# Pieces of each scan group laid between the next group's projection units, and the residual gate's matrix-vector product moved into the first half of the output projection

## The chip, the cores and the metric

The kernel runs on one core of a Trainium2 chip. The metric is the device time of one execution in microseconds (us). One core has five instruction streams, each executed in order: PE (TensorE, matrix products), DVE (VectorE), ACT (ScalarE), POOL (GpSimd) and SP (SyncE, which here only issues DMA transfers). Engines wait for each other by semaphores.

## The reference, cut to what matters

One layer with 512 latent tokens, 256 context tokens and model width 2048. The normalised, modulated input goes through one projection; its columns feed a windowed attention (16 heads) and a bidirectional Mamba-2 scan (16 heads in 4 groups, chunks of 128 tokens). Both results are normalised, multiplied by one output matrix, scaled by a residual gate and added to the input.

```python
shift, scale, gate = jnp.split((jax.nn.silu(c) @ w_mod + b_mod)[:, None, :], 3, axis=-1)
px = (rmsnorm(x, norm_g) * (1 + scale) + shift) @ w_in
...
# scan, per group and direction
cb = jnp.einsum('bclgn,bcsgn->bgcls', cc, bc)
wts = cb[:, :, None] * jnp.exp(segsum(a_t))
y_diag = jnp.einsum('bgrcls,bcsgrp->bclgrp', wts, xdt)
states = jnp.einsum('bclgn,bgrcl,bclgrp->bcgrpn', bc, decay_states, xdt)
...
y_off = jnp.einsum('bclgn,bcgrpn,bgrcl->bclgrp', cc, prev, jnp.exp(a_cs))
...
h = jnp.concatenate([rmsnorm(att * jax.nn.silu(g_att), att_norm_g), rmsnorm(y * jax.nn.silu(z), ssd_norm_g)], axis=-1)
x = x + gate * (h @ w_out)
```

`gate` is one row of 2048 numbers: a vector of 2048 times a matrix of 2048 x 2048 (16 MB in float32).

## The kernel before, in words

**Products.** Every float32 operand is split in two parts, hi and lo, and a product is three matrix multiplications (hi by hi, lo by hi, hi by lo), all through the helper of L49. All elementwise operations of two tensors go through L55.

**Streamed units.** The input projection is cut into units of 128 output columns. `load_unit` (L298) loads a unit's weights in two halves (tile `wr`, 512 KB each); ACT takes the hi part (`wh`, L308) and DVE the lo part (`wl`, L55). `proj` (L316) multiplies 16 blocks by 512 latent tokens (`pj`, 48 matmuls) and, where the unit is wanted for the context, by 256 context tokens (`pjc`, 48 more). In the names `pj_13` or `wr_13_0` the first number is the unit. Unit 0 is the last eighth of the scan's output gate z; units 1 to 16 are the four scan groups (x0, x1, B, C each; C without context); 17 and 18 are the keys, the rest queries and attention gates.

**Scan groups.** `ssd_group` (L474) is called four times. It projects the group's four units, convolves them (`conv_silu`), and then: transposes x and B to token layout (`xtp`, `btp`, to `xtok`, `btok`); forms the chunk states (`stc`, `stx`, with `xw` and `stt` on DVE); forms `cbp`; and, for two pairs of heads, the state term `z` and the diagonal term `yps`. In front of a `yps` stands a chain: a row of running sums is loaded onto all partitions (tile `df`, 256 KB, from `csd` in HBM), ACT takes its exponential (`ec`), DVE the masked differences (L566, four per row), ACT the exponential (L569) and a scaling (L573), DVE the sum of both directions (L575, four) and the product with `cb`. `yps` multiplies the result by `xtok`. The pairs are numbered 0 to 7; `yps_5` is the second pair of group 2.

**Order.** A scheduler lays the instructions of each engine in an order by priorities. Loads and splitting of weights have a raised priority (`HP_W`), as have `df` loads (`HB`) and convolutions, so the next group's projection matmuls come between the pieces of a scan group as far as the scheduler's own order brings them.

**Residual gate.** `gate_step` (L274) is called four times per unit in units 2 to 17. Each call loads one block of 128 x 512 of the gate's weights (tile `wg`, 256 KB, one buffer) and DVE adds the product with the conditioning vector to `ga` (L290). After 16 blocks `gp` sums `ga` over the partitions (a 1 x 512 matmul result), and the row goes to HBM (`grow`). In the output projection it is loaded back onto all partitions (`gate`).

**Output projection.** It has two halves: half 1 (scan's columns of h) first, then half 0 (attention's). In each half four column blocks n of 512 are made; a block loads four `wo` tiles (512 KB, eight k steps of 128), splits them into `woh` and `wol`, and does 12 matmuls per k step into four token tiles (`o_half_n_t`, 96 matmuls a block). Half 1 leaves `part = o * rsum`. After block n of half 1, `add_x` (L799) on POOL makes `part * gate + x` of block n-1, with four `xo` loads of x. Half 0 then makes `o * rsum * gate` (L879) and adds it to `part` on DVE. `finish_half` (L642) of the attention's half (squares on ACT, `hfu` on DVE, `hacc` and `hal` on POOL) runs beside the first block of half 1.

Of the kernel before, what the change touches and what calls it, by code (L numbers as in the profile page):

```python
# [43 lines left out]
def emit(tc, xin, ctxT, wmod, wgate, bgate, wz, wvd, wu, wo, fng, vecs, cst, rope, out, dbg=None):  # L44
# [18 lines left out]
    with es:  # L63
# [24 lines left out]
        # persistent activations: transposed normalised inputs in two exact parts  # L88
# [27 lines left out]
        def rms_rows(o, acc, n, tag):  # L116
            """1 / rms of every token, on all partitions, from the sums of squares per partition."""
# [13 lines left out]
        def load_latent():  # L131
            """Latent tokens: transposed as they come, in column blocks; 1 / rms of every token on all partitions."""
# [44 lines left out]
        # silu of the two modulation vectors, zero-padded to one column group  # L177
# [90 lines left out]
        dp = es.enter_context(tc.tile_pool(name="dp", bufs=1, space=bass.MemoryType.DRAM))  # L268
        grow = dp.tile([1, D], F32, name="grow")
        gsteps = iter(range(4 * KT))  # L270
        gacc = []
        geng = nc.vector

        def gate_step(ld):  # L274
            """One k block of 512 gate columns: products per partition, summed over partitions after the last."""
            i = next(gsteps, None)
            if i is None:
                return
            n, k = divmod(i, KT)
            if k == 0:  # L280
                ga = wp.tile([P, 512], F32, tag="ga", name=f"ga_{n}", bufs=1)
                gacc.append(ga)
                nc.gpsimd.memset(ga, 0.0)
                with tc.issue_after(ld.ins):
                    nc.sync.dma_start(ga[0:1, :], bgate[:, n * 512:(n + 1) * 512])
            ga = gacc[n]
            wg = wp.tile([P, 512], F32, tag="wg", name=f"wg_{n}_{k}", bufs=GB)
            with tc.issue_after(ld.ins):
                nc.sync.dma_start(wg, wgate[n, k])
            geng.scalar_tensor_tensor(out=ga, in0=wg, scalar=sc0[:, k:k + 1], in1=ga, op0=ALU.mult, op1=ALU.add)  # L290
            if k == KT - 1:
                gp = bank("tp", f"gp_{n}", shape=(1, 512))
                mm(gp, ones[:, 0:1], ga, True, True)
                nc.scalar.activation(ga[0:1, :], gp, AF.Copy)
                nc.sync.dma_start(grow[:, n * 512:(n + 1) * 512], ga[0:1, :])

# [1 line left out]
        def load_unit(u, ctxp=False):  # L298
            """Yields (k, hi, lo) weight blocks [128, 128] of unit u."""
            for hf in range(2):  # L300
                with tc.high_priority(HP_W):
                    wr = wp.tile([P, 8, P], F32, tag="wr", name=f"wr_{u}_{hf}", bufs=WR)
                    ld = nc.sync.dma_start(wr, wu[u, :, hf * 8:hf * 8 + 8, :])
                for qf in range(2):
# [6 lines left out]
                    if 2 <= u < 18:  # L311
                        gate_step(ld)
# [3 lines left out]
        def proj(u, with_ctx):  # L316
# [72 lines left out]
        z7, _ = proj(0, False)  # L389
        stmp = sp.tile([P, S], F32, tag="stmp", name="stmp_7")  # L390
        silu2(z7, yT[7], stmp)
        st.close()

# [35 lines left out]
        da = w2("da", "sm", 4, fl)  # L429
# [13 lines left out]
        dd = w2("dd", "sm", 4, fl)  # L443
# [6 lines left out]
        csx = w2("csx", "sm", 4, [P, NT, 2, 16])  # L450
# [8 lines left out]
        def conv_silu(pa, pb, ci, o):  # L459
            """Depthwise conv of width 3 and silu: pa [128, n] in PSUM -> o in SBUF."""  # L460
# [13 lines left out]
        def ssd_group(g, units):  # L474
            ux0, ux1, ub, uc = units
            xs = []
            for i, u in enumerate((ux0, ux1)):
                a, b = proj(u, True)
                o = w2(f"xs_{g}_{i}", "xs", 3, (P, S + CT))
                conv_silu(a, b, 2 * g + i, o)  # L480
                xs.append(o)
            a, b = proj(ub, True)
            bT = w2(f"bT_{g}", "xs", 3, (P, S + CT))
            conv_silu(a, b, 8 + g, bT)
            a, _ = proj(uc, False)
            cT = w2(f"cT_{g}", "cT", 1)
            conv_silu(a, None, 12 + g, cT)

            xtok = w2(f"xtok_{g}", "xtok", 1, (P, 6, 256))
# [32 lines left out]
            for stp in range(3):  # L522
                for d in range(2):
# [7 lines left out]
                    tt(nc.vector, stt_[d][:, nx, :], stt_[d][:, nx, :], sp_, ALU.add)  # L531

            cbp = bank("tp", f"cbp_{g}")
            for c in range(NT):
                cc = slice(c * P, (c + 1) * P)
                mm(cbp[:, cc], bT[:, cc], cT[:, cc], True, True)
            cb = w2(f"cb_{g}", "cb", 1)
            nc.scalar.activation(cb, cbp, AF.Copy, scale=0.25)

            for pr in range(2):  # L540
                tix = 2 * g + pr
                # state term of both heads at once: exp(cs) scales it afterwards
                zs = []
                for d in range(2):
                    z = bank("sa", f"z_{tix}_{d}")
                    for c in range(NT):
                        cc = slice(c * P, (c + 1) * P)
                        mm(z[:, cc], stt_[d][:, c, pr * P:(pr + 1) * P], cT[:, cc], True, True)
                    zs.append(z)
                ecs = [w2(f"ec_{tix}_{d}", "ec", 3) for d in range(2)]  # L550
                yps = bank("pv", f"yps_{tix}")
                dm = []
                for hh in range(2):
                    r = tix * 2 + hh
                    hr = slice(hh * 64, hh * 64 + 64)
                    dx = []
                    for d in range(2):
# [3 lines left out]
                        with tc.high_priority(HB):  # L561
                            nc.sync.dma_start(df, csd[d * 16 + r].partition_broadcast(P))
# [447 lines left out]
```

## Time and profile before

| what | value |
|---|---|
| time before, median of 3 runs (lowest, highest) | 1056.57 us (1055.89, 1059.32) |
| span of the profiled execution | 1054.8 us |
| PE busy | 1009.6 us (96%) |
| DVE busy | 722.0 us (68%) |
| ACT busy | 494.6 us (47%) |
| POOL busy | 173.5 us (16%) |
| moved by DMA | 143.25 MB |

The span of the profiled execution is its own time, from its first instruction to its last; no other time is shown for that execution, and the median of the three runs is 1.8 us above it. In the rows below a group of instructions reads: line, engine, operation, result <- operands, shape and count, then busy time and the mean duration in ns, then the idle time of the engine just before the instructions of this group and what ended it. Matmuls overlap on PE, so one lasts longer than the distance from it to the next.

### The profile page before, as it was taken

The page shows a single profiled execution, that of the slowest core. Times are in us where ns is not written, and L with a number is a line of the kernel's source. Part 1 is how long each engine was busy: PE and PEld are TensorE (multiplying, and loading weights), DVE is VectorE, ACT ScalarE, POOL GpSimd, SP SyncE. Part 2 cuts the span into 40 slices and gives each one's busy share as a digit, 9 for nine tenths or more (in the row PEclk, how much of TensorE's full clock was granted, in tenths as well). Part 3 has the DMA queues.
Part 4 walks back from the last instruction along what each step waited for, and adds up shares of the span by engine and source line. Part 5 has one row for each costly group of instructions (what it writes and reads, how often), then busy time and mean ns, then how long its engine had stood idle before and what let it go on. Part 6 is the DMA issues. An engine that isn't in the chain of part 4 may idle for free.

```text
span 1054.8 us, 15524 instructions
## 1 busy us (share of the span) xinstructions
PE 1009.6 (96%) x5682; PEld 818.7 (78%) x5682; DVE 722.0 (68%) x1474; ACT 494.6 (47%) x1064; POOL 173.5 (16%) x120
## 2 busy tenths in 40 slices
PE   5999999999999989989989999999999998999996
PEld 4677789788778868868868777777777777888885
DVE  4332378585875985885889888788798866333765
ACT  6222275263352453263345567666666655333333
POOL 1232200000210110110037100000000008744220
PEclk9999999999999999989999999999999999999998
DMA  9999963354244244444331211112111135442304
GB/s 333 385 347 348 343 212 95 110 165 147 70 120 145 92 149 125 112 120 139 120 107 56 84 61 42 59 40 80 41 40 61 61 99 221 151 167 91 100 33 160
DMA packets 50845, 143.25 MB, mean 136 GB/s; under 512 B 5544, under 2 KB 5928, under 8 KB 50512
## 3 DMA queue, kind: packets, MB, share of 16 engines
q1 hardware_dynamic: 50768, 142.25, 40.5%
q8 instruction: 45, 0.74, 0.3%
q14 instruction: 32, 0.26, 0.1%
HBM read 137.96 MB, written 4.27 MB: 135 GB/s over the span
## 4 chain that ended last, share of the span: by engine, by line
PE 61%; DVE 12%; DMA 5%; ACT 3%; issue 3%; POOL 1%; SPq 0%; ACTq 0%; DVEq 0%; POOLq 0%
PE pj L49 25%; PE o L49 14%; PE pjc L49 5%; PE pv L49 3%; PE ptp L756 3%; PE sl L49 3%; DMA wg<-in_wgate_dram 2%; PE vps L49 2%; DVE df L566 2%; DVE wl L55 2%; DMA df<-csd 2%; PE sc L49 2%; DVE ga L290 1%; DVE df L575 1%; PE stx L49 1%
## 5 line engine op out<-in xcount | busy, mean ns | idle before, releaser
L49 PE MATMUL pj<-xh,wh 128*128 128x512 f32 x560 | 225.5, 403 | 0.0
L49 PE MATMUL pj<-xl,wh 128*128 128x512 f32 x560 | 224.6, 401 | 0.0
L49 PE MATMUL pj<-xh,wl 128*128 128x512 f32 x560 | 224.0, 400 | 0.0
L308 ACT ACTIVATE wh<-wr 128x512 fp32r<-128x512 f32 x140 | 87.9, 630 | 137.5 <-PE pjc L49 66.2
L49 PEld LDWEIGHTS pj<-xh,wl 128*128 128x128 f32 x560 | 105.7, 189 | 21.3 <-issue 0.9
L55 DVE TENSOR_TENSOR wl<-wr,wh 128x512 fp32r<-128x512 f32 x140 | 103.5, 742 | 24.9 <-ACT wh L308 21.0
L49 PEld LDWEIGHTS pj<-xl,wh 128*128 128x128 f32 x560 | 106.4, 190 | 15.1 <-issue 1.9
L49 PEld LDWEIGHTS pj<-xh,wh 128*128 128x128 f32 x560 | 106.5, 190 | 13.9 <-issue 1.0
L55 DVE TENSOR_TENSOR wol<-wo,woh 128x512 fp32r<-128x512 f32 x56 | 53.3, 968 | 63.6 <-ACT woh L846 57.3
L290 DVE SCALAR_TENSOR_TENSOR ga<-wg,sc,ga 128x512 f32<-128x512 f32 x64 | 50.8, 794 | 49.2 <-DMA wg<-in_wgate_dram 48.1
L55 POOL TENSOR_TENSOR ec<-ec,ec 128x512 f32<-128x512 f32 x8 | 11.2, 1397 | 349.2 <-DVE ec L55 328.9
L846 ACT ACTIVATE woh<-wo 128x512 fp32r<-128x512 f32 x56 | 34.8, 630 | 70.8 <-PE o L49 62.3
L55 POOL TENSOR_TENSOR hacc<-hacc,hsq 128x512 f32<-128x512 f32 x14 | 20.4, 1454 | 288.7 <-ACT hsq L654 286.3
L49 PE MATMUL pjc<-chq,wh 128*128 128x256 f32 x224 | 65.2, 291 | 2.1 <-DVE xs L468 2.1
L49 PE MATMUL pjc<-clq,wh 128*128 128x256 f32 x224 | 64.4, 288 | 0.0
L49 PE MATMUL pjc<-chq,wl 128*128 128x256 f32 x224 | 63.7, 284 | 0.0
L760 ACT ACTIVATE ph<-ptp 128x512 fp32r<-128x512 f32 x72 | 41.1, 597 | 28.2 <-PE ptp L756 26.8
L49 PE MATMUL o<-woh,hsh 128*128 128x512 f32 x128 | 50.9, 397 | 3.1 <-ACT part L865 3.1
L55 DVE TENSOR_TENSOR pl<-ptp,ph 128x512 fp32r<-128x512 f32 x72 | 48.4, 683 | 7.8 <-ACT ph L760 7.4
L566 DVE SCALAR_TENSOR_TENSOR df<-df,cs,cs_sb 128x128 f32<-128x128 f32 x128 | 48.3, 433 | 4.6 <-ACT ec L563 4.5
L49 PEld LDWEIGHTS pjc<-chq,wh 128*128 128x128 f32 x224 | 42.2, 189 | 11.5 <-ACT ec L563 1.6
L55 POOL TENSOR_TENSOR wsl<-wsr,wsh 128x896 fp32r<-128x896 f32 x16 | 33.9, 2116 | 101.0 <-ACT wsh L231 95.7
(282 smaller groups left out, 2341.8 us busy)
## 6 DMA issues: line engine op xcount, KB each, us to landing
wr<-in_wu_dram SPq DMA_DIRECT2D x70, 512.0 KB, 3.9
wm<-in_wmod_dram SPq DMA_DIRECT2D x64, 512.0 KB, 7.5
wg<-in_wgate_dram SPq DMA_DIRECT2D x64, 256.0 KB, 2.6
wo<-in_wo_dram SPq DMA_DIRECT2D x32, 512.0 KB, 4.5
df<-csd SPq DMA_DIRECT2D x32, 256.0 KB, 4.1
wsr<-in_wz_dram SPq DMA_DIRECT2D x16, 448.0 KB, 6.6
wr_v<-in_wvd_dram SPq DMA_DIRECT2D x16, 288.0 KB, 2.9
xt<-in_xin_dram SPq DMA_DIRECT2D x8, 512.0 KB, 7.5
```

The lines of the kernel that those rows point to most:

```text
L49: return nc.tensor.matmul(o, l, r, start=start, stop=stop)
L55: eng.tensor_tensor(out=o, in0=a, in1=b, op=op)
L290: geng.scalar_tensor_tensor(out=ga, in0=wg, scalar=sc0[:, k:k + 1], in1=ga, op0=ALU.mult, op1=ALU.add)
L308: nc.scalar.activation(wh, rr, AF.Copy)
L566: nc.vector.scalar_tensor_tensor(out=df[:, cc], in0=bc[:, cc], scalar=cs[:, d, c, r:r + 1], in1=mF if d == 0 else mB, op0=ALU.subtract, op ...
L575: nc.vector.scalar_tensor_tensor(out=dx[0][:, cc], in0=df[:, cc], scalar=dtt[:, d, c, r:r + 1], in1=dx[0][:, cc], op0=ALU.mult, op1=ALU.add)
L756: nc.tensor.transpose(tp[:, i * P:(i + 1) * P], pt[i][:, n * P:(n + 1) * P], ident)
L760: nc.scalar.activation(ph, tp, AF.Copy)
L846: nc.scalar.activation(wh, wr[:, i, :], AF.Copy)
```

## The change

The scan group becomes five functions, called in an order written out by hand. `stream(g, i)` projects and convolves unit i of group g; `tokens(g)` makes `cbp` and the transposes; `states(g)` the chunk states; `front(g, pr)` the state term and the chain of pair pr up to the masked products; `back(g, pr)` its `yps` and what follows. Tiles `xs` and `bT` take four named slots in turn in place of three rotating buffers; the small dt tiles use the `df` buffers. Unit 0, which stood ahead of the first group, is projected in the last group.

The gate leaves the units. In half 1 of the output projection each k step calls `gate_products`: a load of 512 KB (two blocks of 128 x 512) into one of two `wg` buffers, and two DVE steps that add into `gate`. `gate_sum(n)` multiplies by a 128 x 128 matrix of ones, which leaves the sum on all partitions. `gate` is not written to HBM. `add_x` goes; half 0 makes `part + o * rsum`, times gate, plus x, on DVE. `wo` tiles have 3 buffers in place of 4, their parts 5 in place of 6.

```diff
-        z7, _ = proj(0, False)
...
-                    if 2 <= u < 18:
-                        gate_step(ld)
...
+                if mid is not None and k == KT // 2:
+                    mid()
...
+        for i in range(4):
+            stream(0, i)
+        tokens(0)
         for g in range(4):
-            ssd_group(g, [U0 + 4 * g + i for i in range(4)])
+            if g < 3:
+                stream(g + 1, 0, lambda: states(g))
+            else:
+                states(g)
+            front(g, 0)
+            if g < 3:
+                stream(g + 1, 1)
+            else:
+                z7, _ = proj(0, False)
+                silu2(z7, yT[7], w2("stmp_7", "cve", 1))
+            back(g, 0)
+            front(g, 1)
+            if g < 3:
+                stream(g + 1, 2)
+            back(g, 1)
+            if g < 3:
+                stream(g + 1, 3)
+                tokens(g + 1)
...
+        nc.gpsimd.memset(gate, 0.0)
+        nc.sync.dma_start(gate[0:1, :], bgate)
+
+        def gate_products(i, ld):
+
+            n, k2 = divmod(i, 8)
+            wg = fp.tile([P, 2, 512], F32, tag="wg", name=f"wg_{n}_{k2}", bufs=2)
+            with tc.issue_after(ld.ins):
+                nc.sync.dma_start(wg, wgate[n, 2 * k2:2 * k2 + 2].rearrange("k p c -> p k c"))
+            gn = gate[:, n * 512:(n + 1) * 512]
+            for k in range(2):
+                nc.vector.scalar_tensor_tensor(out=gn, in0=wg[:, k, :], scalar=sc0[:, 2 * k2 + k:2 * k2 + k + 1], in1=gn,
+                                               op0=ALU.mult, op1=ALU.add)
+
+        def gate_sum(n):
+            gn = gate[:, n * 512:(n + 1) * 512]
+            gp = bank("pv", f"gp_{n}")
+            mm(gp, ones, gn, True, True)
+            nc.scalar.activation(gn, gp, AF.Copy)
...
+                        if half == 1:
+                            gate_products(n * 8 + k, ld)
+                        if (half, k) == (1, 2) and n > 0:
+                            gate_sum(n - 1)
+                        if (half, n, k) == (0, 0, 2):
+                            gate_sum(3)
...
-                if half == 1 and n > 0:
-                    add_x(n - 1)
...
+                if half == 0 and n == 2:
+
+                    for t in range(NT):
+                        p3 = part[:, t, 1536:2048]
+                        tt(nc.vector, p3, p3, gate[:, 1536:2048], ALU.mult)
+                        tt(nc.vector, p3, p3, load_x(3, t), ALU.add)
...
-                    tmp = fp.tile([P, 512], F32, tag="xo", name=f"lt_{n}_{t}", bufs=4)
-                    nc.vector.scalar_tensor_tensor(out=tmp, in0=ops[t], scalar=rsum[:, 0, t:t + 1],
-                                                   in1=gate[:, nn], op0=ALU.mult, op1=ALU.mult)
+                    tmp = load_x(n, t)
+                    nc.vector.scalar_tensor_tensor(out=pt_, in0=ops[t], scalar=rsum[:, 0, t:t + 1],
+                                                   in1=pt_, op0=ALU.mult, op1=ALU.add)
+                    tt(nc.vector, pt_, pt_, gate[:, nn], ALU.mult)
                     tt(nc.vector, pt_, pt_, tmp, ALU.add)
```

Where the instructions now stand. The rows that follow are the two programs' instruction lists, one engine at a time; 128x512 is the shape of the result. First PE in the scan, before the change, where group 2's second pair is multiplied while unit 13 (the x0 of group 3) streams; the sum of the gate's third part stands right behind it.

```order
L49 MATMUL pjc_13_4301<-chq3_306,wh_13_1_1_4399 128x256
L49 MATMUL pjc_13_4301<-clq3_1648,wh_13_1_1_4399 128x256
L49 MATMUL yps_5_4234<-df_11_0_4260,xtok_2_4053 64x128
L49 MATMUL yps_5_4234<-df_10_0_4235,xtok_2_4053 64x128
...
L49 MATMUL gp_2_4406<-ga_2_3690,ones_67 1x512
L49 MATMUL pjc_13_4301<-chq3_306,wl_13_1_1_4401 128x256
```

There 62 matmuls of unit 13 stand between `yps_4` and `yps_5`. The same place after the change: the first pair stands behind the last matmul of unit 14, and the state term of the second pair and the whole of unit 15 (96 matmuls) follow before `yps_5`.

```order
L49 MATMUL pjc_14_4116<-clq3_1647,wh_14_1_1_4205 128x256
L49 MATMUL pjc_14_4116<-chq3_306,wl_14_1_1_4207 128x256
L49 MATMUL yps_4_4243<-df_9_0_4087,xtok_2_3838 64x128
L49 MATMUL yps_4_4243<-df_8_0_4062,xtok_2_3838 64x128
...
L49 MATMUL z_5_0_4256<-cT_2_3824,stt_2_0_3934 128x128 x4
L49 MATMUL z_5_1_4261<-cT_2_3824,stt_2_1_3935 128x128 x4
L49 MATMUL pj_15_4321<-xh0_75,wh_15_0_0_4325 128x512
L49 MATMUL pj_15_4321<-xl0_360,wh_15_0_0_4325 128x512
```

So it is in groups 0 to 2, with 96 matmuls of a unit ahead of each `yps`. In group 3, which has no next group, 6 matmuls of unit 0 stand between `z_6` and `yps_6`, and 50 matmuls of unit 17 (keys) between `z_7` and `yps_7`.

Second, DVE in the first block of half 1, before the change: behind the last `hfu` come the lo parts of the weights and nothing else.

```order
L657 TENSOR_SCALAR hfu_0_6_9320<-at3_5345,v_sb_62 128x512
L657 TENSOR_SCALAR hfu_0_7_9327<-at3_5345,v_sb_62 128x512
L55 TENSOR_TENSOR wol_1_1_6_8897<-wo_1_1_3_8894,woh_1_1_6_8896 128x512
L55 TENSOR_TENSOR wol_1_1_7_8913<-wo_1_1_3_8894,woh_1_1_7_8912 128x512
L55 TENSOR_TENSOR wol_1_2_0_8956<-wo_1_2_0_8953,woh_1_2_0_8955 128x512
```

After the change the first gate step stands behind `hfu_0_6`, and gate steps alternate with the lo parts from there to the end of half 1.

```order
L668 TENSOR_SCALAR hfu_0_6_9189<-at3_5124,v_sb_62 128x512
L827 SCALAR_TENSOR_TENSOR gate_8419<-wg_0_0_8435,sc0_124,gate_8419 128x512
L55 TENSOR_TENSOR wol_1_0_7_8578<-wo_1_0_3_8555,woh_1_0_7_8577 128x512
L827 SCALAR_TENSOR_TENSOR gate_8419<-wg_0_0_8435,sc0_124,gate_8419 128x512
L668 TENSOR_SCALAR hfu_0_7_9196<-at3_5124,v_sb_62 128x512
L827 SCALAR_TENSOR_TENSOR gate_8419<-wg_0_1_8455,sc0_124,gate_8419 128x512
...
L827 SCALAR_TENSOR_TENSOR gate_8419<-wg_0_3_8497,sc0_124,gate_8419 128x512 x2
L827 SCALAR_TENSOR_TENSOR gate_8419<-wg_0_4_8519,sc0_124,gate_8419 128x512 x2
L55 TENSOR_TENSOR wol_1_1_5_8715<-wo_1_1_2_8692,woh_1_1_5_8714 128x512
L827 SCALAR_TENSOR_TENSOR gate_8419<-wg_0_5_8539,sc0_124,gate_8419 128x512 x2
L55 TENSOR_TENSOR wol_1_1_6_8737<-wo_1_1_3_8734,woh_1_1_6_8736 128x512
```

PE reads the first finished quarter of the gate in block 1, behind the fourth matmul of k step 4 (52 matmuls into the block); the second and third stand at the same place of blocks 2 and 3, the fourth behind k step 3 of half 0's first block.

```order
L49 MATMUL o_1_1_0_8601<-wol_1_1_4_8695,hsh2_5164 128x512
L49 MATMUL o_1_1_1_8602<-woh_1_1_4_8694,hsh2_5164 128x512
L49 MATMUL gp_0_8657<-gate_8419,ones_67 128x512
L49 MATMUL o_1_1_1_8602<-woh_1_1_4_8694,hsl4_5172 128x512
L49 MATMUL o_1_1_1_8602<-wol_1_1_4_8695,hsh2_5164 128x512
```

Third, SP's queue beside block 3 of half 1, before and after. Before, `wo` loads have x loads (`xo`, 256 KB) between them; after, gate loads of 512 KB, each of which waits for its buffer in front of the `wo` load behind it.

```order
L835 DMA wo_1_3_0_9113<-in_wo_dram 128x1024
L835 DMA wo_1_3_1_9147<-in_wo_dram 128x1024
L804 DMA xo_2_0_9250<-in_xin_dram 128x512
L804 DMA xo_2_1_9254<-in_xin_dram 128x512
L835 DMA wo_1_3_2_9181<-in_wo_dram 128x1024
```

```order
L863 DMA wo_1_3_2_9050<-in_wo_dram 128x1024
L824 DMA wg_2_0_8790<-in_wgate_dram 128x2x512
L824 DMA wg_2_1_8810<-in_wgate_dram 128x2x512
L824 DMA wg_2_2_8832<-in_wgate_dram 128x2x512
L863 DMA wo_1_3_3_9092<-in_wo_dram 128x1024
L824 DMA wg_2_3_8855<-in_wgate_dram 128x2x512
```

## Rows read from the trace of the kernel before

**Rows 1.** The page: busy us of each engine, share of the span, instructions.

```profile
PE 1009.6 (96%) x5682; PEld 818.7 (78%) x5682; DVE 722.0 (68%) x1474; ACT 494.6 (47%) x1064; POOL 173.5 (16%) x120
```

**Rows 2.** Busy time by stretch, granted PE clock, DMA share, GB/s.

```profile
215.00:295.00 80.00, 76.11 (x436) 63.94 (x435) 60.68 (x131) 36.75 (x72) 5.91 (x5) 0.98 0.40 127
295.00:379.00 84.00, 79.76 (x464) 67.56 (x463) 65.76 (x131) 36.44 (x70) 10.13 (x9) 1.00 0.41 127
379.00:464.00 85.00, 78.64 (x445) 65.15 (x446) 65.09 (x130) 34.69 (x67) 7.45 (x7) 0.97 0.43 124
464.00:549.00 85.00, 81.01 (x456) 67.41 (x456) 65.21 (x128) 35.15 (x68) 10.53 (x9) 0.97 0.38 114
865.00:955.00 90.00, 86.90 (x376) 69.94 (x375) 41.52 (x43) 37.06 (x63) 56.99 (x40) 1.00 0.51 181
955.00:1046.00 91.00, 91.00 (x420) 74.64 (x418) 55.46 (x85) 33.85 (x73) 23.86 (x16) 1.00 0.26 86
```

**Rows 3.** PE's waits: who released it, total us, times, longest.

```profile
PE yps L49 <- DVE df L55: 13.6, 4, 4.0
...
PE o L49 <- ACT part L865: 3.1, 1, 3.1
PE pjc L49 <- DVE xs L468: 2.1, 2, 1.2
PE gp L49 <- DVE ga L290: 1.9, 1, 1.9
```

**Rows 4.** The chain that ended last: start, us, what.

```profile
183.56 10.99 PE pj L49 x47
...
318.24 1.43 PE pjc L49 x12
...
890.49 87.77 PE o L49 x375
```

**Rows 5.** DVE's groups in the scan, 215 to 548 us.

```profile
L566 DVE SCALAR_TENSOR_TENSOR df<-df,cs,cs_sb 128x128 f32<-128x128 f32 x128 | 48.3, 433 | 4.6 <-ACT ec L563 4.5
L290 DVE SCALAR_TENSOR_TENSOR ga<-wg,sc,ga 128x512 f32<-128x512 f32 x60 | 47.8, 797 | 47.9 <-DMA wg<-in_wgate_dram 46.8 <-issue 1.0
L575 DVE SCALAR_TENSOR_TENSOR df<-df,dtt,df 128x128 f32<-128x128 f32 x64 | 20.4, 376 | 3.3 <-ACT df L569 3.2
```

**Rows 6.** PE's groups in the scan, 215 to 548 us: the gate's sums.

```profile
L49 PE MATMUL gp<-ga,ones 128*1 128x512 f32 x8 | 5.6, 796 | 1.9 <-DVE ga L290 1.9
```

**Rows 7.** DVE's timeline: a gate step, and the next on the same buffer.

```profile
340.14 0.75 DVE L290 SCALAR_TENSOR_TENSOR ga<-wg,sc,ga 128x512 f32<-128x512 f32 x1 [1.16 <-DMA wg<-in_wgate_dram]
...
344.17 0.75 DVE L290 SCALAR_TENSOR_TENSOR ga<-wg,sc,ga 128x512 f32<-128x512 f32 x1 [2.39 <-DMA wg<-in_wgate_dram]
```

**Rows 8.** The page: DMA issues, count, KB each, us to landing.

```profile
wr<-in_wu_dram SPq DMA_DIRECT2D x70, 512.0 KB, 3.9
wm<-in_wmod_dram SPq DMA_DIRECT2D x64, 512.0 KB, 7.5
wg<-in_wgate_dram SPq DMA_DIRECT2D x64, 256.0 KB, 2.6
wo<-in_wo_dram SPq DMA_DIRECT2D x32, 512.0 KB, 4.5
```

**Rows 9.** Landing times of the loads of tile `wo`.

```profile
DMA to landing us min/median/max: 3.4/4.5/7.2
```

**Rows 10.** PE's timeline where half 1 begins and in its first block.

```profile
863.26 0.39 PE L49 MATMUL o<-woh,hsh 128*128 128x512 f32 x1
...
890.49 0.50 PE L49 MATMUL o<-woh,hsh 128*128 128x512 f32 x1 [3.10 <-ACT part L865]
```

**Rows 11.** DVE's timeline: `hfu` of the attention's half.

```profile
869.11 1.51 DVE L657 TENSOR_SCALAR hfu<-at,v_sb 128x512 f32<-128x512 f32 x1 [1.32 <-POOL hacc L55]
...
879.66 1.51 DVE L657 TENSOR_SCALAR hfu<-at,v_sb 128x512 f32<-128x512 f32 x1
882.36 1.50 DVE L657 TENSOR_SCALAR hfu<-at,v_sb 128x512 f32<-128x512 f32 x1 [1.19 <-POOL hacc L55]
```

More of the change, by code (lines that the diff above doesn't have):

```diff
@@ L268, in emit @@
         dp = es.enter_context(tc.tile_pool(name="dp", bufs=1, space=bass.MemoryType.DRAM))
[L269 to L295, printed above, removed]
         def load_unit(u, ctxp=False):
@@ L472, in conv_silu, with stream, tokens @@
             silu2(o, o, e)
[L474 to L487, printed above, removed]
+        U0 = 8 - NZ
+        slots = ["xs0", "xs1", "xs2", "xs3"]
+        G = [{} for _ in range(4)]
+        def stream(g, i, mid=None):
+            u = U0 + 4 * g + i
+            a, b = proj(u, i < 3, mid)
+            if i == 3:
+                o = w2(f"cT_{g}", "cT", 1)
+            else:
+                sl = slots.pop(0)
+                o = w2(f"xs_{g}_{i}", sl, 1, (P, S + CT))
+                G[g][f"slot{i}"] = sl
+            conv_silu(a, b, (2 * g, 2 * g + 1, 8 + g, 12 + g)[i], o)
+            G[g][i] = o
+        def tokens(g):
+            xs, bT, cT = (G[g][0], G[g][1]), G[g][2], G[g][3]
+            cbp = bank("tp", f"cbp_{g}")
+            for c in range(NT):
+                cc = slice(c * P, (c + 1) * P)
+                mm(cbp[:, cc], bT[:, cc], cT[:, cc], True, True)
+            cb = w2(f"cb_{g}", "cb", 1)
+            nc.scalar.activation(cb, cbp, AF.Copy, scale=0.25)
             xtok = w2(f"xtok_{g}", "xtok", 1, (P, 6, 256))
@@ L505, in ssd_group, with states @@
                                      scale=0.25)
+            G[g].update(xtok=xtok, btok=btok, cb=cb)
+            slots.append(G[g]["slot2"])
+        def states(g):
+            xtok, btok = G[g]["xtok"], G[g]["btok"]
             hs = slice(4 * g, 4 * g + 4)
@@ L597, in emit @@
-        U0 = 8 - NZ
-        for g in range(4):
-            ssd_group(g, [U0 + 4 * g + i for i in range(4)])
+                for hh in (1, 0):
+                    hl = pr * 2 + hh
+                    mmo(yps[hh * 64:hh * 64 + 64, cc], xtok[:, c, hl * HD:hl * HD + HD], dm[hh][:, cc], True, True)
+            yt = w2(f"yt_{tix}", "cve", 1)
+            nc.vector.scalar_tensor_tensor(out=yt, in0=xs[:, 0:S], scalar=dskh[:, tix:tix + 1], in1=yps,
+                                           op0=ALU.mult, op1=ALU.add)
@@ L797, in emit, with load_x @@
         nring = 0
-        def add_x(n):
-            nn = slice(n * 512, (n + 1) * 512)
-            for t in range(NT):
-                xo = fp.tile([P, 512], F32, tag="xo", name=f"xo_{n}_{t}", bufs=4)
-                nc.sync.dma_start(xo, xin[t * P:(t + 1) * P, nn])
-                tt(nc.gpsimd, part[:, t, nn], part[:, t, nn], gate[:, nn], ALU.mult)
-                tt(nc.gpsimd, part[:, t, nn], part[:, t, nn], xo, ALU.add)
+        def load_x(n, t):
+            xo = fp.tile([P, 512], F32, tag="xo", name=f"xo_{n}_{t}", bufs=4)
+            nc.sync.dma_start(xo, xin[t * P:(t + 1) * P, n * 512:(n + 1) * 512])
+            return xo
+        nc.gpsimd.memset(gate, 0.0)
[8 more added lines that the diff above has]
+                nc.vector.scalar_tensor_tensor(out=gn, in0=wg[:, k, :], scalar=sc0[:, 2 * k2 + k:2 * k2 + k + 1], in1=gn,
+                                               op0=ALU.mult, op1=ALU.add)
+        def gate_sum(n):
[3 more added lines that the diff above has]
+            nc.scalar.activation(gn, gp, AF.Copy)
         ssf = fp.tile([P, NT, 4], F32, name="ssf")
@@ L833, in emit @@
                     wpool = fp if deep else wp
[L834 to L835 removed]
+                    wr = wpool.tile([P, 2, 512], F32, tag="wr", name=f"wo_{half}_{n}_{kp}", bufs=3 if deep else WR)
+                    ld = nc.sync.dma_start(wr, wo[half, n, kp])
                     for i in range(2):
@@ L854, in emit @@
                     nc.sync.dma_start(fg, fng.partition_broadcast(P))
-                if half == 1 and n == 1:
-                    nc.sync.dma_start(gate, grow[0].partition_broadcast(P))
-                if half == 1 and n > 0:
-                    add_x(n - 1)
                 if half == 0 and n == 0:
                     half_rstd(a_acc, 0)
-                    add_x(3)
+                if half == 0 and n == 2:
[3 more added lines that the diff above has]
+                        tt(nc.vector, p3, p3, load_x(3, t), ALU.add)
                 nn = slice(n * 512, (n + 1) * 512)
```

137 lines of the change are left out of this document (65 added, 72 removed).

## The prediction

> **What bounds the kernel now.** I read the page first: PE is busy for 96% of the span, far ahead of DVE's 68% [rows 1]. So the time is PE's columns, which the change leaves as they are, plus the places where PE stands or runs at a lower clock. The table by stretch shows where. In the scan, 215 to 549 us, PE is busy 76.11 + 79.76 + 78.64 + 81.01 = 315.5 of 334 us: 18.5 us idle. The granted clock is 0.98, 1.00, 0.97 and 0.97 there, which is worth 80 x 0.02 + 85 x 0.03 + 85 x 0.03 = 6.7 us more [rows 2]. In half 1 of the output projection 3.1 us are idle (865 to 955), in half 0 nothing [rows 2]. The table of PE's waits names the idle time: `yps` for its masked products, four times, 13.6 us; `pjc` for a convolution, 2.1; `gp` for the last gate step, 1.9; and one wait of 3.1 for the copies of `part` in half 1 [rows 3]. The chain that ended last is PE's own matmuls in long runs, and gives their pace: `pj` 10.99 / 47 = 0.234 us each, `pjc` 1.43 / 12 = 0.119, `o` 87.77 / 375 = 0.234 [rows 4]. A unit with context is therefore 48 x 0.234 + 48 x 0.119 = 16.9 us, a block of the output projection 96 x 0.234 = 22.5. What DVE and the DMA queue can deliver beside this is the question, above all for the gate, which gets a new place.
>
> **The scan.** Four waits of 13.6 us are 3.4 each, and the longest is 4.0 [rows 3]. In front of a late `yps` stood 62 matmuls of a unit, 62/96 x 16.9 = 10.9 us; so the chain behind it needs some 10.9 + 3.4 = 14.3 us after the previous `yps`. In groups 0 to 2 there are now 96 matmuls, 16.9 us, 2.6 more than is needed: three waits go. In group 3 the second pair has 50 matmuls of unit 17, 8.8 us: 14.3 - 8.8 = 5.5 us stay. Group 3's states have little beside them now, since unit 0's matmuls are mostly spent ahead of them; I put 1 us there. The wait for `gp` goes, because the sum is no longer there. The low clock stands in the stretches with waits, and I let it go with them. Gain: 18.5 + 6.7 - 5.5 - 1 = 18.7. From below, the low clock may stay and another 1.2 of `pjc` may: 18.7 - 6.7 - 1.2 = 10.8, about 11. From above, if group 3's chain runs early: 25. Unit 0 is moved whole (48 matmuls), at no cost to PE. The gate's 60 DVE steps in the scan, 47.8 us busy [rows 5], leave a DVE that was not the bound; they help the chains above and are not counted again. The gate sums are 512 columns before and after and take 5.6 / 4 = 1.4 us each [rows 6]; they only move.
>
> **The 3.1 us in half 1.** They were the copies of block 0, queued on ACT behind the whole chain of the attention's norm; PE's first `o` is at 863.26 and the matmul that waited at 890.49 [rows 10]. After the change those copies stand ahead of the chain's end. Gain 3.1. If a split of weights takes their place on ACT, it is nothing.
>
> **The first gate sum.** PE reaches it 96 + 52 matmuls after the first `o`: 863.3 + 148 x 0.234 = 897.9 on the clock of the kernel before. DVE begins with the gate behind the seventh `hfu`. The third `hfu` is at 869.1, the late ones follow each other at 882.36 - 879.66 = 2.7 [rows 11]; eight splits that stood between them are elsewhere now. So the seventh is at 869.1 + 4 x 2.7 = 879.9 and ends at 881.4. Then come two steps whose data has long landed, with two splits and the eighth `hfu` between them: the second ends at about 888 (four products 2.8, two splits 1.4, the `hfu` 1.5 and its wait up to 1.2). From there each of the two buffers makes round trips: two products, 1.4 (0.75 each, overlapping a little); the load's landing time L; and the handing over. The last is in the rows: a gate step starts at 340.14 and lasts 0.75, and the next on the same buffer starts at 344.17, 3.3 us after its end; a 256 KB load lands in 2.6, so 0.7 is left [rows 7, 8]. The second buffer carries steps 4, 6 and 8, three trips: 888 + 3 x (2.1 + L), and 0.3 to the sum. PE waits 3L - 3.3.
>
> L is what no row has: 512 KB in the two-block form, one load at a time, beside the `wo` stream. The nearest rows are `wr` with 3.9 and `wo` with 4.5, both 512 KB [rows 8]; the fastest `wo` took 3.4 [rows 9]. Half 1 moved 181 GB/s at a share of 0.51 [rows 2]. The gate's 32 loads of 512 KB, 16.8 MB over some 95 us, are 177 more; 12 `xo` loads and the 1 MB gate row, 4.2 MB or 44 GB/s, mostly go: about 310 GB/s, a share of 0.51 x 310 / 181 = 0.87. Between fast and loaded I take the mean of the two medians, L = 4.2, and keep 3.4 and 5.3 as bounds (at a fuller queue `wm` loads of this size took 7.5 [rows 8]). At 4.2 the first sum costs 3 x 4.2 - 3.3 = 9.3 us; at 3.4, 6.9; at 5.3, 12.6.
>
> The Trainium skill, page "DMA: Bandwidth & Descriptors", section "Anatomy of one DMA", gives a fit of 2.0 us plus the bytes at 436 GB/s: an estimate of 2.6 us for 256 KB, which this trace bears out (2.6), and of 3.2 us for 512 KB, which it does not (3.9 and 4.5). By that estimate the first sum would cost 6.3 us and the later ones nothing.
>
> **The three later sums.** Each needs eight more steps, four trips of each buffer: 4 x (2.1 + L), against 22.5 + 1.4 = 23.9 us of PE. At L = 4.2 that is 25.2: 1.3 each, 3.9 in all. Up to L = 3.9 they are free; at 5.3 they cost 3 x 5.7 = 17.1. Behind a waiting gate step stand the lo parts of the next weights on DVE, and behind a waiting gate load the next `wo` load on SP; PE waits for both, but it is the same time, not more, as all of them follow the gate's pace. If PE's clock falls while it stands, as much as in the scan (6.7 beside 18.5), 13 us of waits add 4.7; in half 1 before, 3.1 us of idle left it at 1.00 [rows 2], and I add nothing.
>
> **Half 0.** DVE gets 20 more operations, about 0.7 each, 14 us, on 55.5 busy of 91 [rows 2]; this is hidden while PE works. The four extra gate products of block 2, 2.8 us, come shortly ahead of the last block's epilogue; I let a quarter of them show at the end: 0.7 us (bounds 0 and 2.8). POOL loses 32 operations of `add_x`, off the path.
>
> **The sum.** -18.7 - 3.1 + 9.3 + 3.9 + 0.7 = -7.9 on the profiled execution's 1054.8, so 1046.9; the median of the runs lies 1.8 above that span, so **1049** on 1056.6.
>
> **Rivals.** In L the gate's price is 3L - 3.3 plus, from 3.9 on, 12L - 46.5; the rest of the sum is -21.1.
>
> *The gate stream fits.* Loads land as the fastest `wo` did, 3.4 [rows 9]; only the first sum is late: -21.1 + 6.9 = -14.2, **1042**. For it: a gate load mostly has the queue to itself, and the 256 KB one took 2.6. Against: medians of 3.9 and 4.5. The Trainium skill's fit, above, is on this side: 3.2 us would give about 1042 as well.
>
> *The gate stream paces half 1.* From L = 4.75 the price eats the gain, from 4.96 the kernel is slower by over 0.3%; at 5.3 it is 12.6 + 17.1 - 21.1 = +8.6, **1065**. For it: one buffer pair, a `wo` median of 4.5 already at a lower load, a share of about 0.87 to come. Against: `wo` loads are issued in bursts and wait for each other; gate loads are not.
>
> *The scan's pieces stay late.* DVE is the engine they wait for. A pair's chain is 16 x 0.433 + 8 x 0.376 = 9.9 us of DVE in these two groups alone [rows 5], and with the unit's splits and convolution nearly fills the 16.9 us of a unit. If it is not through in time, half of the waits stay and the clock with them: the scan gives 7 in place of 18.7, and the sum is +3.8, **1060**. Against it: before, DVE also carried the 47.8 us of the gate, and its waits for `wg`, 47.9 us, stood in the same queue [rows 5].
>
> **How the numbers follow.** About 0.3% (3.2 us) is what a measurement of this kernel can tell from no change, so faster is below 1053.4 and slower above 1059.7. The forecast case (L between 3.8 and 4.7, the scan giving 13 to 23) has 0.50, with a range of its own of 1042 to 1056; a fifth of it lies above 1053.4. The stream that fits has 0.22, all faster. The stream that paces has 0.17, nearly all slower. The late scan has 0.11: half of it slower, the rest no change. Faster: 0.40 + 0.22 = 0.62; same: 0.10 + 0.01 + 0.05 = 0.16; slower: 0.16 + 0.06 = 0.22. The range of 8 in 10 is 1037 to 1063: below it the fitting stream with a scan gain of 25, above it the pacing stream.
>
> **What would show it.** In the table of PE's waits, `yps` should fall from 13.6 to about 5, with one wait left, in group 3; the `part` wait of 3.1 should be gone; waits of `gp` and `o` for gate steps and lo parts, in sum about 13, should be new in half 1 (on the new clock from about 865 on). DVE's idle time in half 1 should be put down to `wg` loads, and their landing time should be about 4.2. The granted clock of the scan should be 0.99 or 1.00. The prediction is wrong if gate loads land in over 5 us or in 3.4, if `yps` waits stay in groups 0 to 2, or if the low clock in the scan does not belong to the waits.

## The result, and the profile after

The changed kernel takes 1067.9 us (median of 4 runs, 1064.5 to 1069.7) against 1056.2 for the kernel before: a ratio of 1.0101, 95% interval 1.0077 to 1.0125. It is slower, and by more than the predicted range allowed. The profiled execution spans 1062.7 us, 7.9 more than the one of before.

The page of the changed kernel, busy time of each engine, answers to [rows 1]:

```profile
PE 1012.3 (95%) x5682; PEld 822.2 (77%) x5682; DVE 725.7 (68%) x1494; ACT 495.6 (47%) x1064; POOL 129.6 (12%) x85
```

The changed kernel's busy time by stretch (columns as in [rows 2]); the last two stretches are half 1 and half 0:

```profile
184.00:290.00 106.00, 105.48 (x591) 90.21 (x591) 60.14 (x139) 43.23 (x81) 1.29 (x1) 1.00 0.24 73
290.00:368.00 78.00, 75.95 (x447) 64.76 (x446) 53.76 (x114) 34.90 (x68) 7.95 (x6) 1.00 0.25 82
368.00:449.00 81.00, 77.89 (x446) 67.12 (x445) 54.30 (x114) 34.74 (x67) 7.75 (x6) 0.96 0.24 79
449.00:536.00 87.00, 81.45 (x469) 68.52 (x469) 66.87 (x136) 38.80 (x77) 14.45 (x11) 0.96 0.26 84
849.00:949.00 100.00, 86.53 (x352) 67.17 (x351) 71.30 (x89) 36.85 (x62) 22.41 (x15) 0.95 0.69 238
949.00:1051.00 102.00, 101.05 (x460) 82.17 (x459) 72.40 (x120) 36.69 (x75) 15.96 (x8) 1.00 0.46 152
```

And its table of PE's waits, which answers to [rows 3]:

```profile
PE gp L49 <- DVE gate L827: 11.7, 4, 8.4
PE cbp L49 <- DVE cT L110: 7.7, 3, 3.0
...
PE yps L49 <- DVE df L55: 2.9, 1, 2.9
PE o L49 <- DVE wol L55: 2.7, 1, 2.7
```

Three of the four `yps` waits are gone, as is the one for `part`. New are the long waits of the gate's sums, three of `cbp` for the convolved C, and one of 2.7 us for a lo part. Half 1 has 13.5 us of idle PE and a clock of 0.95; the scan still has 0.96 twice.

The stages show where the time went. They are cut, on PE's timeline, at the end of the last `vps`, the first context score (`sc`) of the attention, the first `o`, and the last matmul; us:

| kernel | to the scan | scan | attention | output projection | after the last matmul | span |
|---|---|---|---|---|---|---|
| before | 183.6 | 403.4 | 276.3 | 182.9 | 8.6 | 1054.8 |
| changed | 184.0 | 389.6 | 275.8 | 201.9 | 11.4 | 1062.7 |
| e1, scan order alone | 186.4 | 408.7 | 275.9 | 184.4 | 9.0 | 1064.4 |
| e2, gate alone | 184.3 | 396.5 | 276.8 | 203.3 | 11.4 | 1072.3 |
| e4, sums late | 182.5 | 386.9 | 276.0 | 193.6 | 11.1 | 1050.1 |
| e5, tokens in mid unit | 182.7 | 381.6 | 275.8 | 203.0 | 11.1 | 1054.1 |
| e10, e4 + e5 + e7 | 182.8 | 381.6 | 275.9 | 192.1 | 8.6 | 1041.1 |
| e12, gate alone, mended | 183.7 | 394.4 | 276.8 | 192.9 | 8.6 | 1056.3 |

The change wins 13.8 us in the scan (5.6 of which are the sums' own columns, which moved out) and loses 19.0 in the output projection and 2.8 behind it. Each row is one execution. The scan's code is the same in the changed kernel, e4, e6 and e7, and took 389.6, 386.9, 389.7 and 389.6 us, so a difference of under 3 us between two rows of this column shows little.

How the first sum comes to wait, in the chain of the changed kernel that ended last (start, us, what):

```profile
868.31 1.77 DVE gate L827
...
871.68 1.76 DVE gate L827
...
877.82 2.48 DVE wol L55 x4
880.30 0.67 DVE gate L827
...
881.78 4.41 DMA wg<-in_wgate_dram
...
889.90 4.84 DMA wg<-in_wgate_dram
...
896.63 2.05 PE gp L49 x2
```

It is the predicted chain: late start, then round trips with loads in flight. And how `cbp` comes to wait, in the same view:

```profile
398.00 2.69 DVE df L549 x2
...
403.91 1.28 ACT df L556 x4
...
406.44 0.74 DVE cT L437
...
408.07 0.64 ACT cve L109
...
408.73 0.70 DVE cT L110
...
409.48 2.08 PE cbp L49 x8
```

The convolution of C takes its turn on ACT and DVE behind the chain of the group's second pair (`df`), and PE, with only 25 matmuls of the next unit ahead of `cbp`, is there 3 us early.

### The profile page after: what moved, and what is told of

Same layout as the page of the kernel before. It is cut to its first block, busy times and chain, and to the rows that moved or that the text cites. A ratio compares the mean times of both kernels' runs of the same rounds, so it can differ in the third digit from the quotient of the medians.

```text
span 1062.7 us, 15446 instructions
## 1 busy us (share of the span) xinstructions
PE 1012.3 (95%) x5682; PEld 822.2 (77%) x5682; DVE 725.7 (68%) x1494; ACT 495.6 (47%) x1064; POOL 129.6 (12%) x85
## 4 chain that ended last, share of the span: by engine, by line
PE 70%; DVE 13%; DMA 7%; ACT 5%; issue 4%; POOL 1%; SPq 0%; ACTq 0%; DVEq 0%; POOLq 0%
PE pj L49 29%; PE zps L49 7%; PE pjc L49 6%; DMA wg<-in_wgate_dram 5%; PE vps L49 4%; PE md L49 3%; PE pv L49 3%; PE o L49 3%; PE ptp L767 3%; PE sl L49 3%; DVE gate L827 2%; DVE df L549 2%; PE sc L49 2%; PE z L49 1%; DVE wl L55 1%
## 5 line engine op out<-in xcount | busy, mean ns | idle before, releaser
L55 DVE TENSOR_TENSOR wl<-wr,wh 128x512 fp32r<-128x512 f32 x140 | 99.7, 714 | 35.5 <-ACT wh L280 34.3
L827 DVE SCALAR_TENSOR_TENSOR gate<-wg,sc,gate 128x512 f32<-128x512 f32 x64 | 51.1, 798 | 24.4 <-DMA wg<-in_wgate_dram 23.2
L549 DVE SCALAR_TENSOR_TENSOR df<-df,cs,cs_sb 128x128 f32<-128x128 f32 x128 | 55.0, 483 | 15.5 <-ACT ec L546 15.4
L55 DVE TENSOR_TENSOR wol<-wo,woh 128x512 fp32r<-128x512 f32 x56 | 44.5, 805 | 21.1 <-ACT woh L874 19.0
L49 PE MATMUL o<-wol,hsh 128*128 128x512 f32 x128 | 52.0, 406 | 2.7 <-DVE wol L55 2.7
L49 PE MATMUL o<-woh,hsl 128*128 128x512 f32 x128 | 52.3, 408 | 0.0
L742 ACT ACTIVATE pe<-sl,nm 128x256 f32<-128x256 f32 (+1 forms) x64 | 33.6, 526 | 35.4 <-DVE nm L740 33.6
```

The lines of the kernel that those rows point to most:

```text
L49: return nc.tensor.matmul(o, l, r, start=start, stop=stop)
L55: eng.tensor_tensor(out=o, in0=a, in1=b, op=op)
L549: nc.vector.scalar_tensor_tensor(out=df[:, cc], in0=bc[:, cc], scalar=cs[:, d, c, r:r + 1], in1=mF if d == 0 else mB, op0=ALU.subtract, op ...
L742: nc.scalar.activation(pe[:, 0:nl * P], sl, AF.Exp, bias=nm[:, i:i + 1], accum_out=sm[:, i, 0:1])
L827: nc.vector.scalar_tensor_tensor(out=gn, in0=wg[:, k, :], scalar=sc0[:, 2 * k2 + k:2 * k2 + k + 1], in1=gn, op0=ALU.mult, op1=ALU.add)
```

## The experiments

Each was timed beside the kernel before; a ratio is to that kernel, with its 95% interval. First, one part of the change at a time.

**e1: the scan's order alone.** The changed kernel with `gate_step` in the units and the output projection of before.

```diff
-                        if half == 1:
-                            gate_products(n * 8 + k, ld)
+                    if 2 <= u < 18:
+                        gate_step(ld)
```

> The scan's new order alone: gate steps in the units and the output projection as before. Theory 1 (the new order saves PE waits by itself, and is robbed of half by its own new wait, cbp for the convolution of C): 1046 to 1049 us, yps waits under 4 us, cbp waits of 7 to 8. Theory 2 (the yps waits went because the gate's 64 steps left DVE, not because of the order): yps waits of 8 or more, 1055 to 1058.

Measured: 1066.9 us, ratio 1.0092 (1.0077 to 1.0108). Neither: the `yps` waits go, so the order removes them by itself, but `cbp` takes more than they gave. From e1's table of PE's waits:

```profile
PE cbp L49 <- DVE cT L110: 19.9, 4, 7.1
...
PE yps L49 <- DVE df L55: 3.3, 1, 3.3
```

The scan is 5.3 us longer than before. With the gate steps on DVE, the convolution of C comes up to 7 us late.

**e2: the gate's move alone.** The scan as before without gate steps; the output projection of the change.

```diff
-                    if 2 <= u < 18:
-                        gate_step(ld)
...
+                        if half == 1:
+                            gate_products(n * 8 + k, ld)
```

> The gate's move alone: scan in its old order, without gate steps. Theory 1: the gate's new place costs about 17.9 us of PE time in half 1 less 3.1 that go, and 2.8 at the end, and gives back only the gp wait of 1.9: 1070 to 1074. Theory 2 (DVE without gate steps frees the old scan too): yps waits fall from 13.6 to under 6, 1061 to 1066.

Measured: 1074.1, ratio 1.0170 (1.0148 to 1.0191): theory 1, at its upper end. The old scan keeps its `yps` waits without the gate on DVE (13.8 us in four). The two parts don't add up: their scans change by +5.3 and -6.9, both together by -13.8. Of the last two, 5.6 are the sums' columns, which only moved; without them they are -1.3 and -8.2. Each part needs the other.

**e3: cbp half a unit later.** In the changed kernel, the `cbp` products move from `tokens` to the start of `states`.

```diff
         def tokens(g):
-            cbp = bank("tp", f"cbp_{g}")
...
         def states(g):
+            cbp = bank("tp", f"cbp_{g}")
...
```

> The changed kernel with the four cbp products of a group made where its states begin, half a unit later. Theory 1: the three cbp waits, 7.7 us, go and nothing takes their place: 1059 to 1061; if the granted clock of 0.96 in groups 1 and 2 belongs to these waits, 6 us more, 1054. Rival: DVE is behind in the scan, and the wait moves to the transposes or yps: 1066 to 1068.

Measured: 1066.7, ratio 1.0095 (1.0078 to 1.0111): the rival. Its table of PE's waits:

```profile
PE xtp L473 <- ACT xtok L475: 9.0, 3, 3.2
```

Three waits again, now at the transposes: PE waits for ACT's copies of the first ones, and these stand on ACT behind the convolution of C (in group 2 the convolution starts there at 405.96, the copies at 406.62).

**e4: the gate's sums late.** All four in half 0's first block; nothing reads the gate earlier.

```diff
-                        if (half, k) == (1, 2) and n > 0:
-                            gate_sum(n - 1)
-                        if (half, n, k) == (0, 0, 2):
-                            gate_sum(3)
+                        if (half, n) == (0, 0) and k >= 4:
+                            gate_sum(k - 4)
```

> The changed kernel with all four gate sums in half 0's first block, k steps 4 to 7. Theory 1a (the sums stand too early, the stream itself is fast enough): gp waits fall from 11.7 to under 2, and half 1 loses about 10 us: 1056 to 1059. Theory 1b (the gate stream paces DVE, and the lo parts of the weights stand behind its steps): PE's wait moves from gp to o for wol, at least 8 us of it, and to the first sum in half 0; 1064 to 1068.

Measured: 1057.0, ratio 0.9996 (0.9975 to 1.0017): theory 1a. The output projection is 8.3 us shorter than in the changed kernel. In e4's tables, PE's waits and DVE's:

```profile
PE o L49 <- DVE wol L55: 3.3, 3, 2.7
...
PE gp L49 <- DVE gate L827: 2.1, 1, 2.1
```

```profile
DVE gate L827 <- DMA wg<-in_wgate_dram: 27.8, 21, 3.2
```

DVE stands for gate loads as long as ever (23.2 us in the changed kernel), and PE no longer cares: the lo parts are made far enough ahead. What hurt was a matmul in PE's own order that needed the end of a quarter of the stream.

**e5: tokens in mid unit.** In the changed kernel, `cbp` and the transposes move to k step 7 of the next unit, the states from k step 8 to 11. In group 3, which has no next unit, they stay directly ahead of the states.

```diff
-                stream(g + 1, 0, lambda: states(g))
+                stream(g + 1, 0, {7: lambda: tokens(g), 11: lambda: states(g)})
```

> The changed kernel with each group's cbp and transposes in k step 7 of the next unit (42 of its matmuls ahead, 25 in the change) and the states in k step 11. e3 showed that moving cbp alone moves the wait to the transposes, behind ACT's copies. Theory 1 (PE reaches this place too early; what it needs comes 2 to 3 us later, whatever stands first): 17 more matmuls, 3.0 us, take the three waits of 7.7 us in sum: 1058 to 1061, and the clock of 0.96 in groups 1 and 2 returns. Rival (DVE and ACT are behind in these units as a whole): the waits turn up at stc, z or yps, 1066 to 1068.

Measured: 1056.5, ratio 1.0001 (0.9979 to 1.0022), better than theory 1, although only two of the three waits went. E5's busy time by stretch, columns as above; the stretches hold `cbp` of groups 1, 2 and 3:

```profile
290.00:368.00 78.00, 77.98 (x474) 67.01 (x475) 55.73 (x118) 36.24 (x70) 7.94 (x6) 1.00 0.26 82
368.00:449.00 81.00, 80.75 (x477) 69.23 (x477) 59.21 (x122) 36.41 (x69) 8.95 (x7) 1.00 0.28 91
449.00:530.00 81.00, 75.25 (x420) 63.13 (x420) 61.93 (x128) 36.59 (x72) 13.29 (x11) 0.96 0.27 84
```

PE is busy throughout, and the clock is at 1.00, except in the last stretch, where group 3's `cbp` (2.9 us) and `yps` (2.9) still wait. A move that only passes the wait on (e3) and one that covers it (this) differ in the matmuls put ahead.

**e6: gate loads of 256 KB in four buffers** in place of 512 KB in two, in the changed kernel.

```diff
-            wg = fp.tile([P, 2, 512], F32, tag="wg", name=f"wg_{n}_{k2}", bufs=2)
+                wg = fp.tile([P, 512], F32, tag="wg", name=f"wg_{n}_{kk}", bufs=4)
```

> The changed kernel with gate loads of 256 KB in four buffers, the same room as two of 512 KB. Theory 1 (a buffer's round trip paces the stream): four trips of about 0.75 + 0.7 + 3 us in flight give a step every 1.1 us, less than PE's 1.4; the three later gp waits (1.4, 0.9, 0.95) go and the first falls from 8.4 to 4 or 5: 1061 to 1064. Rival (the DMA queues' share of 0.7 to 0.9 in half 1 is the limit): loads of 256 KB land in over 3.5 us, and the gp waits stay within 2 us of 11.7: 1067 to 1070.

Measured: 1062.5, ratio 1.0049 (1.0032 to 1.0066): theory 1's time, and its three later waits are gone; the first is 7.0, where 4 or 5 was forecast. From its table of PE's waits, and ACT's timeline:

```profile
PE gp L49 <- DVE gate L828: 7.0, 1, 7.0
...
PE o L49 <- ACT part L901: 3.1, 1, 3.1
```

```profile
880.27 0.63 ACT L875 ACTIVATE woh<-wo 128x512 fp32r<-128x512 f32 x1 [4.46 <-DMA wo<-in_wo_dram]
880.81 2.40 ACT L901 ACTIVATE part<-o,rsum 128x512 f32<-128x512 f32 x4
```

Only the first sum is late, though loads of 256 KB land in 3.7 us at the median, as the rival said they would: with four in flight that is enough. And the wait for `part` is back, 3.1 us as in [rows 3], but for another reason: the copies stand on ACT behind a split whose `wo` load was late.

**e7: x and the gate of the fourth column block earlier,** in the changed kernel: after half 0's second block.

```diff
-                if half == 0 and n == 2:
+                if half == 0 and n == 1:
```

> The changed kernel with the gate and x of the fourth column block (eight DVE operations) after half 0's second block instead of the third. Theory 1 (DVE's queue at the end is 5 us behind PE because these eight stand in the last stretch): the distance from PE's last matmul to the end falls from 11.4 to about 8.6 us, 1064 to 1066. Rival (the epilogue of the third block alone, longer by eight operations than before, is what is behind): 11 us stay, 1067 to 1069.

Measured: 1065.0, ratio 1.0064 (1.0039 to 1.0088); 8.6 us from the last matmul to the end: theory 1.

**e8: e4, e5, e6 and e7 together.**

> The changed kernel with the edits of e4, e5, e6 and e7 together. If the prices add up (e4 measured 1057; less 7.7 for cbp, less 2.8 at the end): 1045 to 1048, about 1% faster than the kernel before. If they cover each other: 1050 to 1056.

Measured: 1043.5, ratio 0.9868 (0.9846 to 0.9890). The prices add up, and more.

**e9: no gate loads.** E1, with one gate block loaded and read by all 64 steps; the other 63 loads are left out.

```diff
-            wg = wp.tile([P, 512], F32, tag="wg", name=f"wg_{n}_{k}", bufs=GB)
-            with tc.issue_after(ld.ins):
-                nc.sync.dma_start(wg, wgate[n, k])
+            if not gw:
+                gw.append(wp.tile([P, 512], F32, tag="wg", name="wg_0", bufs=GB))
+                nc.sync.dma_start(gw[0], wgate[n, k])
+            wg = gw[0]
```

> e1 (new scan order, gate steps in the units) with the gate's first block loaded once and all 64 steps reading it; 63 gate loads and so the right gate are left out. Theory A (DVE stands still for gate loads, 19.7 us in e1's scan, and the chains and convolutions that PE waits for stand behind): cbp waits fall from 19.9 to about 8, 1050 to 1055 us. Theory B (it is the work of the steps on a DVE that is nearly full beside a pair's chain): cbp waits stay over 14, 1061 to 1067.

Measured: 1063.4, ratio 1.0055 (1.0035 to 1.0075). From its table of PE's waits:

```profile
PE cbp L49 <- DVE cT L110: 14.0, 3, 5.5
...
PE pjc L49 <- DVE xs L471: 5.2, 4, 2.2
```

At the edge of theory B: the loads are worth 6 us of e1's `cbp` waits, 3.9 of which come back at `pjc`; the scan, cut as above, takes 407.1 us, only 1.6 less than e1's. So most of what e1's scan loses is lost when no step waits for a load. That leaves the steps' own work on DVE as the cause; it is argued by exclusion, for no run takes away this work and keeps the loads.

**e10: e8 with 512 KB loads in two buffers** (the changed kernel with e4, e5 and e7).

> e8 without e6's edit: gate loads of 512 KB in two buffers, the sums late. Theory 1 (once no sum waits for the stream, its pace is not on the path): the same as e8 within 2 us, 1042 to 1046. Rival (the slower stream still holds the weights' lo parts behind it on DVE): o waits for wol of 5 us or more, 1047 to 1050.

Measured: 1044.2, ratio 0.9876 (0.9855 to 0.9896): theory 1; once no sum waits, the size of the loads is worth nothing that these runs can tell. The output projection is still 9.2 us longer than before, 5.6 of them the sums' columns. The `wo` buffers, which the change cuts from 4 to 3, were not tested apart; PE's longest wait for a lo part (2.7 us) is in half 1's first block, which does not use them.

**e11: e1 with the edit of e5.**

> e1 with the edit of e5: cbp and transposes in k step 7 of the next unit, gate steps in the units, output projection as before. If the extra lateness in e1 is a fixed time per group (5 us more than in the change, each), 17 matmuls take 3 us of each wait: cbp waits of 8 to 11, 1054 to 1058. Rival: with the gate steps every later step of the group is late too, and the waits go on to stc, z or yps: 1062 to 1067.

Measured: 1059.8, ratio 1.0025 (1.0012 to 1.0038), between the two: `cbp` waits 14.5 us in three. With 17 more matmuls ahead, the convolution is still late by up to 5.9.

**e12: e2 with the edits of e4 and e7.**

> The old scan order with the gate's move as mended (e2 with the edits of e4 and e7). If the stages add up: the scan as in e2 (6.9 us less than before), the output projection as in e10 (192.1 us against 182.9 before), the end as before: +2.3 us, 1057 to 1061, so the gate's move alone, even mended, gains nothing. Rival (the old scan's yps waits and the gate's stalls are the only losses, and the mended move gains by itself): 1052 or less.

Measured: 1058.9, ratio 1.0013 (0.9995 to 1.0031): the stages add up. The gate's move, mended, is worth nothing without the new scan order; e11 says nearly the same of the order without the move (0.25% slower).

## Why the prediction was wrong

By stages, predicted against measured, with the 5.6 us of the sums counted where they stand: scan -24.3 against -13.8; output projection +15.7 against +19.0; behind the last matmul +0.7 against +2.8; the rest 0 against -0.1. The span was missed by 15.8 us, and 10.5 of them are the scan. Without the sums' columns the scan gave 8.2 where the forecast was 18.7 and its lower bound 11.

**The scan: the step that failed is "three waits go", with nothing put in their place.** I looked for the old wait in the new order and found it covered, which held (one `yps` wait of 2.9 is left; I had 5.5). I did not ask what the other pieces of the group now stood behind. `tokens` follows the convolution of C directly, 25 matmuls into the next unit, and that convolution stands on ACT and DVE behind the second pair's chain. The new `cbp` waits, 7.7 us, bring the scan's idle time, over the first four stretches above, to 0.5 + 2.1 + 3.1 + 5.6 = 11.2 where I had 6.5. The rival "the pieces stay late" had the right engine, DVE, and nearly the right gain, 7 us, but the wrong piece, `yps`.

**The low clock: the step "I let it go with them" failed too.** 0.96 over 81 and 87 us is 6.7 us lost, as much as before. In e5, where the waits of groups 1 and 2 are covered, it is 1.00 there, and the scan's idle time is 0.5 + 0.0 + 0.3 + 5.8 = 6.5, what I had forecast for the change. The idle time, 4.7 more than forecast, and the clock, 6.7, make up for the 10.5 missed and 0.9 more. But a wait does not always bring the low clock. E4 has the changed kernel's scan and its `cbp` waits (8.0 us), and in its execution the stretch of group 2, 3.1 us of it idle, stayed at 1.00:

```profile
368.00:449.00 81.00, 77.92 (x469) 66.31 (x467) 54.88 (x115) 36.42 (x70) 7.79 (x6) 1.00 0.24 79
```

So part of the 6.7 is the luck of the one execution, and why the clock falls at one wait and not at another stays open.

**The gate: the mechanism was right, the price in part by luck.** Waits of `gp` and `wol` are 14.4 us where I had 13.2: first sum 8.4 (9.3), the other three 3.3 together (3.9), landing time 4.5 (4.2). But at the measured 4.5 my formulas give 10.2 and 7.5, so errors met inside them. The second load's steps end at 877.9, 28.5 us after the first `o` at 849.4, not 24.7, since DVE's steps take up to 1.77 beside POOL where I had 0.75; and PE reached the sum 38.8 us after it, not 34.6, held by a lo part for 2.7 and slowed by a granted clock of 0.50, the lower of its two levels, from 872.6 to 876.0. The queues' share in half 1 was 0.69 where I had 0.87. Not in the sum were PE's low clock (0.95 in half 1; I had weighed it and added nothing) and the slower matmuls around each sum.

The Trainium skill's fit (page "DMA: Bandwidth & Descriptors", section "Anatomy of one DMA — SWDGE (gpsimd) path", an estimate of 3.2 us for 512 KB) would have made the later sums free. The page gives it for DMAs issued by GpSimd; the loads here are issued by SP. They took 4.5 us at the median and 3.4 at the least, and all three later sums waited.

**The 3.1 us for `part`** left the table, but were not gained. The copies start no earlier than before, 26.6 us after the first `o` against 26.5 (863.26 before, 849.39 after); PE comes later, since it now waits 2.7 for a lo part ahead of them. ACT before, then PE and ACT after:

```profile
889.77 2.40 ACT L865 ACTIVATE part<-o,rsum 128x512 f32<-128x512 f32 x4
```

```profile
871.81 0.50 PE L49 MATMUL o<-wol,hsh 128*128 128x512 f32 x1 [2.69 <-DVE wol L55]
```

```profile
875.97 2.40 ACT L900 ACTIVATE part<-o,rsum 128x512 f32<-128x512 f32 x4
```

The step "those copies stand ahead of the chain's end" was wrong: the chain's last copy on ACT (`hah`) starts at 873.87, ahead of them.

**The end: a mis-sized term.** I let a quarter of four gate products show, 0.7; the eight operations showed 2.8, my upper bound, and e7 took exactly that back.

**The median** lies 5.2 us above the profiled span, not 1.8: the profiled execution is the fastest of the four runs. Why the others are 3 to 5 us longer was not settled.

So the ordering of the rivals was wrong as well: "the gate stream paces half 1" gave nearly the right time, 1065, but by luck. The stream cost about what the forecast case said, and the scan gave too little to pay for it.

## What to carry to other kernels

When pieces of work are moved apart to cover one wait, list every matmul that reads a result of another engine and ask of each what now stands ahead of it on PE and ahead of its producer; the wait that was longest is the one that gets covered, and the next shows. A result that is needed late should be consumed late: moving four sums behind the stream they wait for was worth 11 us (1067.9 to 1057.0), twice what a faster stream gave (e6). And two edits can each be a loss, or nothing, and together a gain (alone 1066.9 and 1074.1, alone and mended 1059.8 and 1058.9, together and mended 1044.2), so parts are to be timed apart and together.

## What the runs showed of the hardware

A DVE operation on two operands in SBUF took up to 2.4 times as long beside POOL: in the changed kernel a gate step takes 1.77 us while POOL works on `hacc` and `hal`, and 0.74 where it starts in a gap of POOL's. The two timelines, DVE and then POOL:

```profile
868.31 1.77 DVE L827 SCALAR_TENSOR_TENSOR gate<-wg,sc,gate 128x512 f32<-128x512 f32 x1
...
873.76 0.74 DVE L827 SCALAR_TENSOR_TENSOR gate<-wg,sc,gate 128x512 f32<-128x512 f32 x1
```

```profile
866.82 1.29 POOL L55 TENSOR_TENSOR hal<-hfu,hah 128x512 fp32r<-128x512 f32 x1
868.06 1.47 POOL L55 TENSOR_TENSOR hacc<-hacc,hsq 128x512 f32<-128x512 f32 x1
869.49 1.71 POOL L55 TENSOR_TENSOR hal<-hfu,hah 128x512 fp32r<-128x512 f32 x1
871.17 1.73 POOL L55 TENSOR_TENSOR hacc<-hacc,hsq 128x512 f32<-128x512 f32 x1
873.92 3.43 POOL L55 TENSOR_TENSOR hal<-hfu,hah 128x512 fp32r<-128x512 f32 x2 [1.02 <-DVE hfu L668]
```

The Trainium skill, page "SBUF — State Buffer", section "SBUF: two separate sides", says that a DVE operation with two SBUF inputs and a GpSimd operation that reads SBUF hold their common port pair in turn, each for its whole length. The rows agree: 1.77 is 0.74 and some 1.0 of standing behind a POOL operation of 1.5, and POOL's own (`hal`) lengthen from 1.29 to 1.71.

Most runs of one kernel that are longer have a lower mean granted clock: e12's twelve runs go from 1053.1 us at 0.990 to 1061.7 at 0.982, though one of 1061.4 has 0.987. In the stretches shown here most of those with 3 us or more of idle PE have 0.95 to 0.98, and those of e5 without have 1.00. Not all have it: before, 295 to 379 with 4.2 idle and half 1 with 3.1 were at 1.00 [rows 2], as was e4's stretch above.
